# A two-layer hybrid decoder trunk on one core: differential queries and keys also made by units of seven products, heads of attention in two chains, scores begun up to two blocks ahead

## The chip, the core and the metric

The kernel runs on one core of a Trainium2 chip. The metric is the device time of one execution in microseconds (us), median of three runs. The core has a matrix engine (PE; its weight loads are listed apart as PEld), a vector engine (DVE), a scalar engine (ACT), a general engine (POOL, which here mostly issues DMAs) and a sync engine (SP, which issues the weight DMAs). Each works through its own list of instructions in order and waits for the others by semaphores.

## The reference, cut to what matters

512 tokens of width 2048 pass two layers. The change is in the second, where one input projection `z = h @ w_in` is split by columns among two attention groups, and the results, each gated, go through one output projection.

```python
z = h @ w_in                                   # h = rmsnorm(x), (512, 2048)
c_q, c_kv, k_rope, mla_gate, dq, dk, dv, diff_gate = split_cols(z, ODD_SPLITS)
...                                            # 768, 512, 64, 1024, 1024, 1024, 1024, 1024 columns
y_c = causal_mla_attention(q, k_c, v_c) * silu(mla_gate)      # 8 heads
qd = dq.reshape(B, S, 8, 2, 64)
kd = dk.reshape(B, S, 8, 2, 64)
vd = dv.reshape(B, S, 8, 128)
p = softmax(mask(qd @ kd * 64 ** -0.5))        # two maps per head, blocks of 128 queries
a = p[:, 0] - lam * p[:, 1]
od = rmsnorm(a @ vd, subln) * (1 - LAMBDA_INIT)
y_d = od * silu(diff_gate)
return concat([y_c, y_d]) @ w_out
```

## The kernel before

Products are made in a format of 32 bits that keeps fewer bits than float32, so every operand is split into a high and a low part (`high` on ACT, line 256, and `low` on DVE, line 259), and every product is three matmuls (`mm3`, line 273): high by high, high by low, low by high. Weights come in pieces of 128 x 1024 by SP's queue (`Piece`, line 283; tile `wr`), and ACT and DVE split each into `wh` and `wl`, two pieces ahead of their use.

**Jobs.** `Job` (line 373) makes 128 output features for all 512 tokens: the weights are the stationary operand, the split input `X1` (tiles `sh`, `sl`) moves, 16 slices of the contraction with three matmuls each, 48 matmuls of 512 columns into one bank `mm`. The result lies features first. The order of the jobs in layer 1 is that in which lines 1314 to 1370 and 1501 to 1506 make them: five gates of the latent attention (MLA), two units, sixteen jobs of the differential heads, six and four latent jobs, the rotary key, three more gates, and then the jobs of the MLA heads.

**Units.** `Unit` (line 1149) makes 1024 output columns at once, tokens first: the input is stationary (128 tokens), the weights move (512 columns), and six of the eight pairs of contraction slices on either side use seven products in place of eight (Strassen's and Winograd's scheme: sums of weights by DVE in `Sum`, line 330; differences of inputs `TS`, tiles `th`, `tl`, made once in `differences`, line 1111). A unit has 348 matmuls of 512 columns; eight jobs have 384. It holds two banks each of `mm`, `o` and `sc`, and in `first` and `second` (lines 1272, 1283) partial sums are read out before a bank is written again. Before the change units make the values (`vd`) and the gate (`gd`) of the differential heads, which `away` (line 1304) scales and stores to DRAM by POOL's queue.

**Attention.** Each head is a task (`diff`, line 984; `mla`, line 1424), whose few matmuls are put between the matmuls of the jobs. For a block of queries, `scores` makes the scores (tile `sc`), DVE takes the maximum (`softmax_max`, an instruction with `p<-sc,cc`), ACT the exponentials and their sum, DVE scales; then PE transposes the result (`pt<-cc,p`, one of 128 x 128 per block of keys), ACT copies it out (`aT`), and PE multiplies it with the values (`o`). At the end of a differential head, POOL takes a power for the norm (`ssq`), DVE makes `osb`, PE transposes it (`pt<-cc,osb`) and ACT makes `y`. The scores of block n + 1 are made between the exponentials and the scaling of block n (line 1014).

**What sets the order.** A planner (`Plan`, line 74) runs while the program is written: it adds up a cost for each instruction (`pe_cost`, line 115, `act_cost`, `dve_cost`, `dma_cost`), keeps a time at which each tile is ready, and resumes a head's task between two steps of a job (three matmuls) once what it waits for is ready by that reckoning. So PE's, ACT's and DVE's lists are fixed when the program is built; POOL's and SP's are ordered by the framework. Work tiles come from one pool of 76 (`wk`, line 219).

Of the kernel before, what the change touches and what calls it, by code (L numbers as in the profile page):

```python
# [73 lines left out]
class Plan:  # L74
# [40 lines left out]
    def pe_cost(self, op, args, kw):  # L115
        if op == "transpose":
            return 0.108
        rhs = args[2]
        n = _free(rhs)
        if rhs.dtype == F32R:  # L120
            return 0.003 + (n / 2400.0 if n >= 256 else 0.213)
        return 0.006 + max(n, 64) * 4 / 2400.0
# [70 lines left out]
def trunk_kernel(ctx: ExitStack, tc, xT, w0, w0o, wg, w1, w1u, wuq, wuk, wuv, w1o, small, cst, outT):  # L193
# [699 lines left out]
    class Output:  # L893


        def __init__(self, wt, Y, res, sink, count, held=0):
            self.Y, self.YS, self.res, self.xr = Y, [None] * 16, res, {}
            self.next, self.upto, self.gap = 0, 16, 0.0
            self.jobs = [big_job(wt, m, self.YS, self.done(m, sink), self.pre(m), None, (False, m < held))
                         for m in range(count)]  # L900
# [5 lines left out]
        def splitter(self):  # L906
            while self.next < 16:
                k = self.next
                while k >= self.upto or self.Y[k] is None:
                    yield plan.now + 0.4  # L910
                yield after(self.Y[k])
                h, l = wk("yh", F32R), wk("yl", F32R)
                high(h, self.Y[k])
                yield after(h)
                low(l, self.Y[k], h)
                self.YS[k] = h, l
                self.Y[k] = None
                self.next = k + 1
                yield plan.now + self.gap
# [64 lines left out]
    def diff(h, st):  # L984
# [27 lines left out]
        yield from scores(0)  # L1012
        for n in range(NB):
            (pp, sums), nk = res.pop(n), (n + 1) * P
            if n < NB - 1:
                yield from scores(n + 1)
# [31 lines left out]
        Y1[h] = y  # L1048

    def diff_jobs(h):  # L1050
        st = {}

        def fetch():
            for x, src in (("v", vd), ("g", gd)):
                st[x] = wk(x)
                pool.dma_start(st[x], src[h])

        def q_done(acc):
            z = evac(acc, n1, "dq")
            st["q"] = []  # L1060
            plan.spawn(stacks(z, st["q"]))

        def k_done(acc):
            z = evac(acc, n1, "dk")
            lo = [wk("kl", F32R), wk("kl", F32R)]
            a = [wk("kh", F32R), wk("kh", F32R)]
            st["kh"], st["kl"] = a, lo

            def f():
                yield after(z)  # L1070
                for c in range(2):
                    r, s = slice(64 * c, 64 * c + 64), slice(64 - 64 * c, 128 - 64 * c)
                    high(a[c][r], z[r])
                    high(a[c][s], z[r])
                    yield after(a[c])
                    low(lo[c][r], z[r], a[c][r])
                    low(lo[c][s], z[r], a[c][r])
                yield from diff(h, st)
            plan.spawn(f())

        big_job(w1, 2 * h, X1, q_done, fetch, n1)
        big_job(w1, 2 * h + 1, X1, k_done, None, n1)

    MG = [None] * 8

    mgd = dp.tile([8, P, S], F32, name="mgd")[:, :, :]
    vd = dp.tile([8, P, S], F32, name="vd")[:, :, :]
    gd = dp.tile([8, P, S], F32, name="gd")[:, :, :]

    def mla_gate_job(h, away):  # L1090
        def done(acc):
            z = evac(acc, n1, "mg")

            def f():
                yield after(z)
                act.activation(z, z, AF.Silu)
                if away:
                    yield after(z)
                    pool.dma_start(mgd[h], z)
                else:  # L1100
                    MG[h] = z
            plan.spawn(f())
        j = big_job(w1, 16 + h, X1, done, None, n1)
        if h == 0:
            j.pre = lambda: plan.spawn(differences())
# [208 lines left out]
    for h in range(5):  # L1314
        mla_gate_job(h, True)
    Unit(w1u[0], away(vd, AF.Identity))
    Unit(w1u[1], away(gd, AF.Silu))
    for h in range(8):
        diff_jobs(h)
# [47 lines left out]
    LQ = Latent(29, 6, C_QN)  # L1367
    LKV = Latent(25, 4, C_KVN)
    big_job(w1, 24, X1, rope_key_done, None, n1)
    for h in range(5, 8):  # L1370
        mla_gate_job(h, False)
# [52 lines left out]
    def mla(h, st):  # L1424
# [4 lines left out]
        if MG[h] is None:  # L1429
            MG[h] = wk("mg")  # L1430
            pool.dma_start(MG[h], mgd[h])
# [27 lines left out]
        yield from scores(0)  # L1459
        for n in range(NB):  # L1460
            (p, sums), nk = res.pop(n), (n + 1) * P
            if n < NB - 1:
                yield from scores(n + 1)
# [37 lines left out]
    for h in range(8):  # L1501
        if h % 4 == 0:
            rope_jobs(h // 4)
            value_jobs(h // 4)
# [17 lines left out]
    O1 = Output(w1o, Y1, x1d, sink1, 16 - TAIL, 2)  # L1522
# [102 lines left out]
def _tiles1():  # L1625

    cq, ckv, kr, mg, dq, dk, dv, dg = 0, 768, 1280, 1344, 2368, 3392, 4416, 5440
    out = []
    for h in range(8):
        for b in (dq, dk):  # L1630
            out.append(_ranges((b + 128 * h, b + 128 * h + 128)))
# [109 lines left out]
```

## Time and profile before

| what | value |
|---|---|
| median of 3 runs | 1547.8 us (1547.55 to 1548.03) |
| the profiled execution | 1547.16 us |
| its span, first to last instruction | 1545.4 us |
| DVE busy | 935.6 us (61%) |
| ACT busy | 728.6 us (47%) |
| POOL busy | 71.3 us (5%) |
| moved by DMA | 179.75 MB, mean 116 GB/s |
| granted PE clock, mean | 0.997 |

The profile is of one execution; the time outside its span is 1.8 us. Its page gives the busy time of each engine and the chain of work that ended last, and its trace can be asked for groups of instructions, for stretches of time, and for the instructions one by one. A matmul's duration there contains the time from its start until its result is out, so that durations of neighbours overlap; what a matmul costs in a row of them is the distance from start to start.

### The profile page before, as it was taken

What the parts mean: (1) busy time and instruction counts of PE and PEld (TensorE: products, weight loads), DVE (VectorE), ACT (ScalarE), POOL (GpSimd) and SP (SyncE); (2) the same over time, 40 slices, a digit from 0 to 9 for tenths busy, and PEclk for the clock granted to TensorE, in tenths of its full rate; (3) what the DMA queues carried; (4) which work ended last, traced back from release to release, by engine and by line L of the source; (5) the groups of instructions that cost most, each with busy time, mean ns of one, the idle gap of its engine ahead of it and who ended that gap; (6) DMA issues with size and microseconds to landing.
All of it is one profiled execution on the core that took longest, in us unless ns stands there. A gap on an engine that the chain in (4) does not pass through costs nothing.

```text
span 1545.4 us, 19462 instructions
## 1 busy us (share of the span) xinstructions
PE 1529.6 (99%) x7346; PEld 1280.0 (83%) x7346; DVE 935.6 (61%) x1741; ACT 728.6 (47%) x1285; POOL 71.3 (5%) x118
## 2 busy tenths in 40 slices
PE   9999999999999999999999999999999999999996
PEld 7888888888888888878888888888888888888886
DVE  7877676677863445675763677666443466743344
ACT  7465455555652333534433556555333456632222
POOL 0000000000000110000002000000000000010000
PEclk9999999999999999999999999999999999999998
DMA  7223222222334444645636322222232322343323
GB/s 285 85 85 97 85 85 86 89 80 83 95 129 136 152 140 163 222 155 177 210 124 206 101 82 82 96 82 83 83 95 89 98 77 66 111 145 101 99 83 110
DMA packets 59487, 179.75 MB, mean 116 GB/s; under 512 B 7024, under 2 KB 11264, under 8 KB 59264
## 3 DMA queue, kind: packets, MB, share of 16 engines
q1 hardware_dynamic: 51776, 153.84, 31.3%
q0 software_dynamic: 7616, 24.66, 4.7%
q8 instruction: 58, 0.95, 0.3%
q14 instruction: 37, 0.30, 0.1%
HBM read 164.58 MB, written 13.89 MB: 115 GB/s over the span
## 4 chain that ended last, share of the span: by engine, by line
PE 96%; issue 2%; DVE 1%; DMA 0%; ACT 0%; SPq 0%; POOLq 0%; POOL 0%; DVEq 0%; ACTq 0%
PE mm L62 78%; PE sc L62 8%; PE o L62 7%; PE pt L62 3%; DMA xin<-in_xT 0%; DVE st L62 0%; ACT wh L62 0%; DVE s L62 0%; SPq L62 0%; DVE wl L62 0%; DVE sl L62 0%; DVE mg L62 0%; DVE wx L62 0%; POOLq L1736 0%; ACT sh L62 0%
## 5 line engine op out<-in xcount | busy, mean ns | idle before, releaser
L62 DVE TENSOR_TENSOR wl<-wr,wh 128x1024 fp32r<-128x1024 f32 (+1 forms) x236 | 280.9, 1190 | 379.1 <-ACT wh L62 374.7
L62 PE MATMUL mm<-sh,wh 128*128 128x512 f32 x1056 | 419.4, 397 | 0.0
L62 ACT ACTIVATE wh<-wr 128x1024 fp32r<-128x1024 f32 (+1 forms) x236 | 243.8, 1033 | 360.7 <-PE mm L62 252.7
L62 PE MATMUL mm<-sl,wh 128*128 128x512 f32 x1056 | 412.1, 390 | 0.0
L62 PE MATMUL mm<-sh,wl 128*128 128x512 f32 x1056 | 412.1, 390 | 0.0
L62 PEld LDWEIGHTS mm<-sh,wl 128*128 128x128 f32 x1056 | 198.2, 188 | 42.8
L62 PEld LDWEIGHTS mm<-sh,wh 128*128 128x128 f32 x1056 | 198.6, 188 | 36.1
L62 PEld LDWEIGHTS mm<-sl,wh 128*128 128x128 f32 x1056 | 198.8, 188 | 35.5
L62 PE MATMUL mm<-yh,wh 128*128 128x512 f32 x448 | 174.9, 390 | 0.0
L62 PE MATMUL mm<-yl,wh 128*128 128x512 f32 x448 | 174.5, 389 | 0.0
L62 PE MATMUL mm<-yh,wl 128*128 128x512 f32 x448 | 174.4, 389 | 0.0
L62 PEld LDWEIGHTS mm<-yl,wh 128*128 128x128 f32 x448 | 84.1, 188 | 17.4 <-DVE yl L62 0.3
L62 PEld LDWEIGHTS mm<-yh,wh 128*128 128x128 f32 x448 | 84.1, 188 | 17.4
L62 PEld LDWEIGHTS mm<-yh,wl 128*128 128x128 f32 x448 | 84.1, 188 | 17.3
L62 ACT ACTIVATE p<-p,negm 128x128 f32<-128x128 f32 (+3 forms) x96 | 53.8, 560 | 60.0 <-DVE negm L62 58.3
L62 DVE CUSTOM_DVE_ANT_0 p<-sc,cc 128x128 f32<-128x128 f32 (+3 forms) x96 | 46.7, 488 | 41.2 <-PE sc L62 40.8
L62 ACT ACT_TABLE_LOAD x36 | 46.2, 1283 | 1.4 <-PEq L1732 0.7
L62 ACT ACTIVATE sq<-xr 128x512 f32<-128x512 f32 (+1 forms) x33 | 19.3, 586 | 55.0 <-DVE xr L62 55.0
L62 ACT ACTIVATE aT<-pt 128x128 f32<-128x128 f32 (+3 forms) x64 | 27.5, 434 | 36.9 <-PE pt L62 36.4
L62 DVE TENSOR_TENSOR ss<-ss,sq 128x512 f32<-128x512 f32 (+1 forms) x54 | 36.0, 667 | 10.2 <-ACT sq L62 9.4
L62 PE MATMUL mm<-ch,wh 128*128 128x512 f32 x104 | 41.7, 401 | 0.0
L62 PE MATMUL mm<-cl,wh 128*128 128x512 f32 x104 | 40.7, 391 | 0.0
(318 smaller groups left out, 2380.2 us busy)
## 6 DMA issues: line engine op xcount, KB each, us to landing
wr<-in_w SPq DMA_DIRECT2D x134, 512.0 KB, 3.5
wr<-in_w0o SPq DMA_DIRECT2D x32, 512.0 KB, 3.5
wr<-in_w1o SPq DMA_DIRECT2D x32, 512.0 KB, 3.5
wr<-in_w1u SPq DMA_DIRECT2D x30, 512.0 KB, 3.9
wx<-in_w1u SPq DMA_DIRECT2D x40, 256.0 KB, 4.8
wr<-in_wuq SPq DMA_DIRECT2D x12, 384.0 KB, 3.1
xin<-in_xT SPq DMA_DIRECT2D x16, 256.0 KB, 5.2
xr<-in_xT POOLq DMA_DIRECT2D x16, 256.0 KB, 4.0
```

Source lines behind the costliest of these rows:

```text
L62: return f(*args, **kw)
```

## The change

- The queries and keys of the differential heads are made by two more units (`qd`, `kd`), ahead of those for `vd` and `gd`, tokens first, and go to DRAM. The sixteen jobs `diff_jobs` are gone.
- `diff_heads` is a chain of four heads, and two chains run, one begun 8 us after the other by the planner's clock. Each head fetches its `q` and `k` by POOL's queue, and PE transposes them to features first (`pt<-cc,q`, `pt<-cc,k`, four of 128 x 128 each) before they are split as before. The heads now run beside the remaining gates, the rotary key and the latent jobs, whose order is changed, and beside the first value jobs of MLA.
- In both attentions the scores are a task of their own (`ahead`), up to one block ahead in a differential head and up to two in an MLA head.
- A finished differential head `y` goes to DRAM (`y1d`) and is fetched again (`yr`) when the output projection splits it; all eight MLA gates go to DRAM and come back.
- The planner's cost of a matmul is changed: 0.2267 us for 512 columns of the split format (before 0.2163), 0.108 at the least.

On PE, the place where the second unit has ended. The names are bank, moving operand, stationary operand; `sh` and `sl` are the input's two parts, `wh` and `wl` the weight's. Before, the first job of the differential queries:

```order
L62 MATMUL mm_6769<-sh_4000,wh_6702 128x512
L62 MATMUL mm_6769<-sl_4001,wh_6702 128x512
L62 MATMUL mm_6769<-sh_4000,wl_6704 128x512
L62 MATMUL mm_6769<-sh_4071,wh_6702 128x512
L62 MATMUL mm_6769<-sl_4072,wh_6702 128x512
L62 MATMUL mm_6769<-sh_4071,wl_6704 128x512
```

Now, a third unit:

```order
L62 MATMUL mm_6776<-wh_6709,sh_4003 128x512
L62 MATMUL mm_6776<-wl_6710,sh_4003 128x512
L62 MATMUL mm_6776<-wh_6709,sl_4004 128x512
L62 MATMUL mm_6777<-wh_6709,sh_4003 128x512
L62 MATMUL mm_6777<-wl_6710,sh_4003 128x512
L62 MATMUL mm_6777<-wh_6709,sl_4004 128x512
```

The operands have changed sides: the input is stationary now, and two banks take turns.

On PE, a place in the middle of the differential heads, where a block's scores, its transposes and its product with the values stand among the rows of a job. Before:

```order
L62 MATMUL pt_7781<-cc_78,p_7633 128x128 x3
L62 MATMUL sc_7788<-kh_7687,qa_7563 128x256
L62 MATMUL sc_7788<-kl_7685,qa_7563 128x256
L62 MATMUL mm_7670<-sh_5005,wh_7601 128x512
L62 MATMUL mm_7670<-sl_5006,wh_7601 128x512
L62 MATMUL mm_7670<-sh_5005,wl_7603 128x512
L62 MATMUL mm_7670<-sh_5092,wh_7601 128x512
L62 MATMUL mm_7670<-sl_5093,wh_7601 128x512
L62 MATMUL mm_7670<-sh_5092,wl_7603 128x512
L62 MATMUL o_7490<-v_7094,aT_7795 128x128 x3
L62 MATMUL sc_7805<-kh_7688,qb_7564 128x256
L62 MATMUL sc_7805<-kl_7686,qb_7564 128x256
```

Now, at the end of one head while another begins (directly above the first row stand `sc_9869<-kl_9767,qb_9736`, the last scores of the block that `p_9855` belongs to, and one matmul of the job):

```order
L62 MATMUL mm_9774<-sl_4939,wh_9689 128x512
L62 MATMUL mm_9774<-sh_4938,wl_9691 128x512
L62 MATMUL pt_9882<-cc_78,osb_9876 128x128 x4
L62 MATMUL sc_9890<-kh_9768,qa_9735 128x256
L62 MATMUL sc_9890<-kl_9766,qa_9735 128x256
L62 MATMUL mm_9774<-sh_5008,wh_9689 128x512
L62 MATMUL mm_9774<-sl_5009,wh_9689 128x512
L62 MATMUL mm_9774<-sh_5008,wl_9691 128x512
L62 MATMUL mm_9774<-sh_5095,wh_9689 128x512
L62 MATMUL mm_9774<-sl_5096,wh_9689 128x512
L62 MATMUL mm_9774<-sh_5095,wl_9691 128x512
L62 MATMUL pt_9913<-cc_78,p_9855 128x128
```

The rows of two heads now alternate within a few matmuls of the job, and the transposes of a block stand closer behind its scores. From the maxima of its second map to the last scaling, that block's rows stand next to each other in DVE's list, with none of another head or of the weights between.

On POOL, the end of a differential head. `ssq` is the power, `v`, `g`, `q` and `k` are fetches from DRAM. Before:

```order
L62 TENSOR_TENSOR ssq_7746<-ssq_7746,nhalf_79 128x4
L62 DMA v_8218<-vd 128x512
L62 DMA g_8220<-gd 128x512
L62 TENSOR_TENSOR ssq_8031<-ssq_8031,nhalf_79 128x4
L62 DMA v_8497<-vd 128x512
```

Now:

```order
L62 TENSOR_TENSOR ssq_8129<-ssq_8129,nhalf_79 128x4
L62 DMA y1d<-y_8527 128x512
L62 DMA q_8534<-qd 128x512
L62 DMA k_8536<-kd 128x512
L62 DMA v_8599<-vd 128x512
L62 DMA g_8601<-gd 128x512
```

The head's result is stored (`y1d`), and the next head's queries and keys are fetched behind it; of the six fetches of queries that follow a head's end, two stand behind a store of `y` in this way and four ahead of it.

The diff, cut to its core:

```diff
...
         rhs = args[2]
         n = _free(rhs)
         if rhs.dtype == F32R:
-            return 0.003 + (n / 2400.0 if n >= 256 else 0.213)
-        return 0.006 + max(n, 64) * 4 / 2400.0
+            return max(0.108, n * 17 / 38400.0)
+        return 0.002 + max(n, 64) * 4 / 2400.0
     TABLES = {AF.Exp: "e", AF.Sigmoid: "s", AF.Sqrt: "q", AF.Silu: "u"}
...
     class Output:
-        def __init__(self, wt, Y, res, sink, count, held=0):
+        def __init__(self, wt, Y, res, sink, count, held=0, away=0):
             self.Y, self.YS, self.res, self.xr = Y, [None] * 16, res, {}
-            self.next, self.upto, self.gap = 0, 16, 0.0
+            self.next, self.upto, self.gap, self.away = 0, 16, 0.0, away
             self.jobs = [big_job(wt, m, self.YS, self.done(m, sink), self.pre(m), None, (False, m < held))
                          for m in range(count)]
...
                 k = self.next
                 while k >= self.upto or self.Y[k] is None:
                     yield plan.now + 0.4
+                if k < self.away:
+                    y, self.Y[k] = self.Y[k], wk("yr")
+                    pool.dma_start(self.Y[k], y)
                 yield after(self.Y[k])
                 h, l = wk("yh", F32R), wk("yl", F32R)
                 high(h, self.Y[k])
...
                 pp.append(p)
             res[n] = pp, sums
-        yield from scores(0)
+        begun = [0]
+
+        def ahead():
+            for n in range(NB):
+                while n > begun[0] + 1:
+                    yield plan.now + 0.3
+                yield from scores(n)
+
+        plan.spawn(ahead())
         for n in range(NB):
+            while n not in res:
+                yield plan.now + 0.3
             (pp, sums), nk = res.pop(n), (n + 1) * P
-            if n < NB - 1:
-                yield from scores(n + 1)
+            begun[0] = n
             yield after(*pp)
             rr = tiny(2, "rr")
             dve.reciprocal(rr, sums)
...
         y = wk("y")
         act.activation(y, t[0], AF.Identity, scale=subs)
         give("pt", t[0])
-        Y1[h] = y
-
-    def diff_jobs(h):
-        st = {}
-
-        def fetch():
-            for x, src in (("v", vd), ("g", gd)):
+        yield after(y)
+        pool.dma_start(y1d[h], y)
+        Y1[h] = y1d[h]
+
+    qd, kd, vd, gd = (dp.tile([8, P, S], F32, name=x)[:, :, :] for x in ("qd", "kd", "vd", "gd"))
+
+    def diff_heads(hs):
+
+        def fetch(st, h, names):
+            for x in names:
                 st[x] = wk(x)
-                pool.dma_start(st[x], src[h])
-
-        def q_done(acc):
-            z = evac(acc, n1, "dq")
+                pool.dma_start(st[x], {"q": qd, "k": kd, "v": vd, "g": gd}[x][h])
+
+        def features_first(z, out):
+            yield after(z)
+            t = []
+            yield from take("pt", t)
+            transposes(t[0], z, range(NB))
+            yield after(t[0])
+            out.append(t[0])
+
+        for h in hs:
+            st, t = {}, []
+            fetch(st, h, ("q", "k"))
+            yield from features_first(st["q"], t)
             st["q"] = []
-            plan.spawn(stacks(z, st["q"]))
-
-        def k_done(acc):
-            z = evac(acc, n1, "dk")
+            yield from stacks(t[0], st["q"])
+            give("pt", t.pop())
+            fetch(st, h, ("v", "g"))
+            yield from features_first(st["k"], t)
+            z = t.pop()
             lo = [wk("kl", F32R), wk("kl", F32R)]
             a = [wk("kh", F32R), wk("kh", F32R)]
+            for c in range(2):
+                r, s = slice(64 * c, 64 * c + 64), slice(64 - 64 * c, 128 - 64 * c)
+                high(a[c][r], z[r])
+                high(a[c][s], z[r])
+                yield after(a[c])
+                low(lo[c][r], z[r], a[c][r])
+                low(lo[c][s], z[r], a[c][r])
+                yield plan.now
+            give("pt", z)
             st["kh"], st["kl"] = a, lo
-
-            def f():
-                yield after(z)
-                for c in range(2):
-                    r, s = slice(64 * c, 64 * c + 64), slice(64 - 64 * c, 128 - 64 * c)
-                    high(a[c][r], z[r])
-                    high(a[c][s], z[r])
-                    yield after(a[c])
-                    low(lo[c][r], z[r], a[c][r])
-                    low(lo[c][s], z[r], a[c][r])
-                yield from diff(h, st)
-            plan.spawn(f())
-
-        big_job(w1, 2 * h, X1, q_done, fetch, n1)
-        big_job(w1, 2 * h + 1, X1, k_done, None, n1)
+            yield from diff(h, st)
     MG = [None] * 8
+    y1d = dp.tile([8, P, S], F32, name="y1d")[:, :, :]
     mgd = dp.tile([8, P, S], F32, name="mgd")[:, :, :]
-    vd = dp.tile([8, P, S], F32, name="vd")[:, :, :]
-    gd = dp.tile([8, P, S], F32, name="gd")[:, :, :]
-
-    def mla_gate_job(h, away):
+
+    def mla_gate_job(h):
         def done(acc):
             z = evac(acc, n1, "mg")
             def f():
                 yield after(z)
                 act.activation(z, z, AF.Silu)
-                if away:
-                    yield after(z)
-                    pool.dma_start(mgd[h], z)
-                else:
-                    MG[h] = z
+                yield after(z)
+                pool.dma_start(mgd[h], z)
             plan.spawn(f())
-        j = big_job(w1, 16 + h, X1, done, None, n1)
+        j = big_job(w1, h, X1, done, None, n1)
         if h == 0:
             j.pre = lambda: plan.spawn(differences())
...
         return sink
     for h in range(5):
-        mla_gate_job(h, True)
-    Unit(w1u[0], away(vd, AF.Identity))
-    Unit(w1u[1], away(gd, AF.Silu))
-    for h in range(8):
-        diff_jobs(h)
+        mla_gate_job(h)
+    for i, (dst, func) in enumerate(((qd, AF.Identity), (kd, AF.Identity), (vd, AF.Identity), (gd, AF.Silu))):
+        Unit(w1u[i], away(dst, func))
+    first_filler = len(jobs)
     class Latent:
         def __init__(self, base, n, gcol):
...
             KR.extend((h, l))
         plan.spawn(f())
-    LQ = Latent(29, 6, C_QN)
-    LKV = Latent(25, 4, C_KVN)
-    big_job(w1, 24, X1, rope_key_done, None, n1)
     for h in range(5, 8):
-        mla_gate_job(h, False)
+        mla_gate_job(h)
+    big_job(w1, 8, X1, rope_key_done, None, n1)
+    LKV = Latent(9, 4, C_KVN)
+    LQ = Latent(13, 6, C_QN)
+
+    def heads_start():
+        for i in range(2):
+            plan.spawn(diff_heads(range(i, 8, 2)), plan.now + 8 * i)
+    jobs[first_filler].pre = heads_start
     qrs = {}
     VC = {}
...
             yield plan.now + 0.4
         q, k, qr = st["q"], st["k"], qrs.pop(h)
         st.clear()
-        if MG[h] is None:
-            MG[h] = wk("mg")
-            pool.dma_start(MG[h], mgd[h])
+        MG[h] = wk("mg")
+        pool.dma_start(MG[h], mgd[h])
         vc = slice((h % 4) * P, (h % 4 + 1) * P)
         v = [VC[h // 4, n] for n in range(NB)]
         o = []
...
             softmax_exp(p, n, negm, sums)
             res[n] = p, sums
-        yield from scores(0)
+        begun = [0]
+
+        def ahead():
+            for n in range(NB):
+                while n > begun[0] + 2:
+                    yield plan.now + 0.3
+                yield from scores(n)
+
+        plan.spawn(ahead())
         for n in range(NB):
+            while n not in res:
+                yield plan.now + 0.3
             (p, sums), nk = res.pop(n), (n + 1) * P
-            if n < NB - 1:
-                yield from scores(n + 1)
+            begun[0] = n
             yield after(p)
             dve.reciprocal(sums, sums)
             dve.tensor_scalar(p[:, :nk], p[:, :nk], sums, None, ALU.mult)
...
     heads = []
     for h in range(8):
         if h % 4 == 0:
+            value_jobs(h // 4)
             rope_jobs(h // 4)
-            value_jobs(h // 4)
         heads.append(len(jobs))
         mla_jobs(h)
...
             yield from n2.add(xr)
         plan.spawn(post())
-    O1 = Output(w1o, Y1, x1d, sink1, 16 - TAIL, 2)
+    O1 = Output(w1o, Y1, x1d, sink1, 16 - TAIL, 2, 8)
     jobs[heads[5]].pre = lambda: O1.start(16, 1.5)
     def finish(half, parts):
...
 def _tiles1():
-    cq, ckv, kr, mg, dq, dk, dv, dg = 0, 768, 1280, 1344, 2368, 3392, 4416, 5440
+    cq, ckv, kr, mg = 0, 768, 1280, 1344
     out = []
-    for h in range(8):
-        for b in (dq, dk):
-            out.append(_ranges((b + 128 * h, b + 128 * h + 128)))
     for h in range(8):
         out.append(_ranges((mg + 128 * h, mg + 128 * h + 128)))
     out.append(_ranges((kr, kr + 64), (kr, kr + 64)))
...
     w0o = _pack(A(l0_w_out), plain, rows0)
     wg = np.ascontiguousarray(np.concatenate([A(l0_gate_x_w), A(l0_gate_a_w)], axis=2))
     w1 = _pack(A(l1_w_in), _tiles1())
-    w1u = np.stack([_pack_quarters(A(l1_w_in), np.arange(c, c + 1024)) for c in (4416, 5440)])
+    w1u = np.stack([_pack_quarters(A(l1_w_in), np.arange(c, c + 1024)) for c in (2368, 3392, 4416, 5440)])
     rows1 = np.concatenate([np.arange(1024, 2048), np.arange(1024)])
     w1o = _pack(A(l1_w_out), plain, rows1)
     uq = A(l1_w_uq)
```

## The prediction

> **What bounds the kernel now.** I read the page first: engines, slices, chain.
>
> ```profile
> span 1545.4 us, 19462 instructions
> PE 1529.6 (99%) x7346; PEld 1280.0 (83%) x7346; DVE 935.6 (61%) x1741; ACT 728.6 (47%) x1285; POOL 71.3 (5%) x118
> ...
> PEclk9999999999999999999999999999999999999998
> ...
> PE 96%; issue 2%; DVE 1%; DMA 0%; ACT 0%; SPq 0%; POOLq 0%; POOL 0%; DVEq 0%; ACTq 0%
> ```
>
> PE is busy for 99% of the span at a full granted clock, and 96% of the chain that ended last is PE. Busy time alone would prove little, since durations of neighbours overlap; so next I read what PE waited for, over the whole run (columns: total us, times, longest).
>
> ```profile
> PE pt L62 <- DVE dg L62: 1.8, 1, 1.8
> PE sc L62 <- DVE s L62: 1.3, 4, 0.4
> PE sc L62 <- DVE junk L62: 1.1, 1, 1.1
> PE pt L62 <- ACT sq L62: 0.8, 1, 0.8
> PE o L62 <- DVE sl L62: 0.5, 2, 0.3
> PE mm L62 <- DVE yl L62: 0.3, 1, 0.3
> ```
>
> That is all: 5.8 us. None of it belongs to the sixteen jobs of queries and keys or to a softmax. So the kernel ends when PE has worked through its list, and a change is worth what it takes out of that list, less the waits that it brings in. Work that leaves or joins another engine counts only by such waits.
>
> **The price of a row.** From the chain, in order of time (start, us, what):
>
> ```profile
> 672.37 2.72 PE mm L62 x12
> ...
> 903.42 6.14 PE mm L62 x27
> ...
> 910.83 0.44 PE pt L62 x4
> ```
>
> Twelve matmuls of 512 columns in a unit take 2.72 us, 0.2267 each; 27 in a job take 6.14, 0.2274 each. Four transposes among the heads displace 0.44 us, 0.11 each.
>
> **Queries and keys out of jobs, into units.** Sixteen jobs of 48 matmuls go: 768 x 0.2267 = 174.1 us (174.6 at the job's price). Two units of 348 come. What a unit takes with its waits shows in the two that are there: the first matmul of each, and the first of the job behind them.
>
> ```profile
> 664.56 0.50 PE L62 MATMUL mm<-wh,sh 128*128 128x512 f32 x1
> ...
> 745.04 0.50 PE L62 MATMUL mm<-wh,sh 128*128 128x512 f32 x1
> ...
> 824.61 0.39 PE L62 MATMUL mm<-sh,wh 128*128 128x512 f32 x1
> ```
>
> 80.5 and 79.6 us, 160.1 together, where 696 x 0.2267 would be 157.8: a unit loses about 1.1 us, in the waits `sc <- DVE s` above (two a unit) and where it takes over its banks. New units keep the same rows around these points, so I let them cost the same: 174.1 - 160.1 = **14.0 us saved** (14.6 with the job's price; 16.3 if the new units lost nothing). What feeds a unit is DVE's and ACT's splitting and SP's weights:
>
> ```profile
> 656.00:735.00 79.00, 78.24 (x343) 63.80 (x342) 51.42 (x73) 31.91 (x46) 4.09 (x6) 1.00 0.53 171
> 735.00:815.00 80.00, 79.33 (x348) 64.74 (x347) 54.16 (x76) 33.47 (x48) 6.54 (x9) 1.00 0.52 168
> ```
>
> The columns are PE, PEld, DVE, ACT and POOL busy with counts, PE's clock, DMA share and GB/s. In the second unit, which also carries the first one's results away, DVE is busy for 54 of 80 us and the DMA engines for 52%. It is no slower than the first, so two more in a row should not fall behind either.
>
> **Transposes.** Eight heads have four for q and four for k: 64 x 0.11 = **7.0 us added**. They stand on PE's list and nothing hides them. A group stands whole among matmuls of a job, as `osb` did.
>
> One rule speaks against this. The Trainium skill, "TensorE: Matmul & The Clock Gate", section "Part 4: PE-mode transpose", gives some 275 ns for a transpose of 128 x 128 in a kernel and says that the array does not count as busy during it. By that, 64 would be an estimated 17.6 us. The chain above disagrees with it as a price in a row, at 0.11 us each, though the duration of one agrees:
>
> ```profile
> L62 PE MATMUL pt<-cc,osb 128*128 128x128 f32 x32 | 4.9, 275 | 0.0
> ```
>
> 275 ns from start to result; in a row the next one starts long before that.
>
> **The fetch of q.** Two of the six later fetches stand on POOL behind the store of the last head's `y`, which waits for ACT. On PE there stand, from the end of that head's `osb` transposes to the new `pt<-cc,q`, 19 matmuls of 512 columns, 3 transposes and 3 fp32 products (two passes of 0.11): 4.31 + 0.33 + 0.66 = 5.3 us. Needed are ACT's `y`, POOL's issue of the store, and a fetch like that of `v`:
>
> ```profile
> L62 ACT ACTIVATE y<-pt,subs x8: 669/688/691, 911.3 to 1089.3; 128x512 f32<-128x512 f32 x8
> ...
> L62 POOL DMA_DIRECT2D x1d<-xr x16 | 8.7, 547 | 168.3 <-DVE xr L62 168.3
> ...
> DMA to landing us min/median/max: 2.9/4.2/5.6
> ```
>
> 0.69 + 0.55 + 4.2 = 5.4 us, between 4.1 and 6.8; so PE waits 0.1 us in the middle, at most 1.5, twice: **0.3 us** (0 to 3). The four other fetches need not wait for `y`, the keys stand 2 us and more further down, and the first two heads' queries were asked for while a unit still ran.
>
> On this fetch the Trainium skill, "DMA: Bandwidth & Descriptors", section "Anatomy of one DMA — SWDGE (gpsimd) path", fits about 2.0 us plus bytes over 436 GB/s, which for 256 KB is an estimated 2.6 us. The wait would then be nothing. No fetch of `v` here was that fast, so the row is used.
>
> **Two chains, scores ahead, another planner cost.** These move rows on PE and neither add nor take any. Their cost is waits that are not there now. The planner had taken a matmul for 0.2163 us where it takes 0.2267, so all that it scheduled came 5% later on PE than it reckoned; that cushion is gone. Counting PE's rows at the prices above between a block's last scores and its transposes, the middle one of 64 blocks has 10.1 us before and 5.4 now, the shortest 3.8 and 2.7. The shortest is shown with the change. Its needs, for 128 keys:
>
> ```profile
> L62 DVE CUSTOM_DVE_ANT_0 p<-sc,cc 128x128 f32<-128x128 f32 x24 | 6.9, 286 | 5.9 <-PE sc L62 5.8
> L62 DVE DVE_READ_ACCUMULATOR2_ANT negm<- 128x1 f32 x160 | 13.3, 83 | 0.0
> L62 ACT ACTIVATE p<-p,negm 128x128 f32<-128x128 f32 x24 | 9.6, 399 | 14.1 <-DVE negm L62 14.0
> L62 ACT ACTIVATION_READ_ACCUMULATOR p<-p,negm 128x1 f32 x96 | 17.9, 187 | 0.0
> L62 DVE RECIPROCAL rr<-sums 128x2 f32<-128x2 f32 x32 | 5.1, 160 | 0.1
> L62 DVE TENSOR_TENSOR rr<-rr,lam 128x1 f32<-128x1 f32 x32 | 5.1, 160 | 1.1
> L62 DVE TENSOR_SCALAR p<-p,rr 128x128 f32<-128x128 f32 x8 | 2.3, 286 | 0.3
> L62 DVE SCALAR_TENSOR_TENSOR p<-p,rr,p 128x128 f32<-128x128 f32 x8 | 2.8, 351 | 0.3
> ...
> L62 DVE TENSOR_TENSOR wl<-wr,wh 128x1024 fp32r<-128x1024 f32 x216 | 263.9, 1222 | 353.3 <-ACT wh L62 348.9 <-PE o L62 4.3
> ```
>
> 1.9 us of work in 2.7 us of PE: enough for four hops between engines, not for a split of weights (1.22 us) ahead of it on DVE. Such a place would wait about 0.5 us, and behind a waiting PE stands everything. I take **0.8 us** in all, a few such places among 64; the bounds are 0 and about 6 us (0.1 us at every block). The end of a head, from its last product through `ssq` and `osb` to the transposes, has 3.2 us at the least now and 3.4 before, where it just sufficed: **0.4 us** (0 to 1).
>
> **A wait that goes.** Before the output projection's last rows PE waited for the last MLA head:
>
> ```profile
> 1371.56 0.49 PE L62 MATMUL mm<-yh,sh 128*128 128x512 f32 x1
> 1372.33 0.50 PE L62 MATMUL mm<-yl,sh 128*128 128x512 f32 x1 [0.27 <-DVE yl L62]
> ```
>
> 0.77 us from start to start where the pitch is 0.23: about 0.5 us lost. The heads now end further ahead of the rows that use them (3.2 us of PE at least, 1.4 before), so **0.5 us** goes. PE's own list is what is late next there. The store and fetch of `y` lie tens of microseconds ahead of `yh`; three more table loads on ACT lie beside PE.
>
> **The sum**, against the profiled execution's 1547.16 us: -14.0 + 7.0 + 0.3 + 0.8 + 0.4 - 0.5 = -6.0, so 1541.2. The median of the runs shown is 0.6 above that execution; I say **1541.5 us**. With every bound at its good end it is -16.3 + 7.0 - 0.5 = -9.8 (1537.4), at its bad end -14.0 + 7.0 + 3 + 6 + 1 = +3 (1550).
>
> **The rivals.** *Softmax waits* (13 in 100): PE meets its transposes too early in both attentions. For it speaks the halved distance; against it that not one such wait is listed now, and that DVE is busy for 61%. At 0.1 us a block, 64 blocks give 6.4 us: 1547, no change. Slower would take over 0.15 us a block.
>
> *Transposes cost their duration* (4): 64 x 0.275 = 17.6 in place of 7.0, so 1541.2 + 10.6 = 1552, slower. It decides from 0.2 us a transpose on. The chain's 0.44 us for four speaks against it. The skill's page named above would have it so.
>
> *Units fall behind* (7): four in a row hold three pairs of banks and take work tiles for sums, results and stores at once. If each new unit lost 3 us more, the end would be 1547.5. Against it speaks the second unit's 79.6 us.
>
> *The saving is not there* (3): if the moving and the stationary operand's change of side mattered, a unit's price would show it, and it does not: 0.2267 against 0.2274.
>
> **How the numbers follow.** The forecast's own case has 73 in 100, between 1538.5 and 1544.5. The range of 8 in 10 takes in most of the first rival and of the third: 1538.5 to 1547.5. About 0.2% (3.1 us) is what a measurement can tell from no change. Faster by more: the forecast and a part of the softmax waits, 0.78. Same: most of the rest of the two rivals, 0.14. Slower: 0.08.
>
> **What would show it.** Right: two more pairs of waits `sc <- DVE s`; units of 80 us each; four transposes of q in 0.44 us in the chain; no wait of `pt` for `p` over a few tenths. Wrong: PE's list of waits with `pt <- DVE p` or `pt <- DMA q` of several us in all, or the third and fourth unit longer than the second.

## The result and the profile after

| | before | after |
|---|---|---|
| median | 1547.67 us (1547.11 to 1548.03) | 1558.2 us (1557.65 to 1558.65, 4 runs) |
| ratio | 1 | 1.007, 95% interval 1.0057 to 1.0083 |
| the profiled execution | 1547.16 us, span 1545.4 | 1557.92 us, span 1556.2 |

The changed kernel is slower by 10.5 us; the forecast was 6 us faster. Its page, the same lines as shown of before:

```profile
span 1556.2 us, 19845 instructions
PE 1527.0 (98%) x7338; PEld 1273.2 (82%) x7338; DVE 995.3 (64%) x1845; ACT 758.5 (49%) x1352; POOL 104.1 (7%) x172
...
PE 85%; DVE 6%; issue 4%; ACT 3%; DMA 1%; SPq 0%; POOL 0%; POOLq 0%; DVEq 0%; ACTq 0%
```

PE is busy for 2.6 us less than before in a span that is 10.8 us longer, and the chain that ended last has lost 11 points of PE to DVE, ACT and issue. So the list of PE did get shorter; PE stands still in it more often. Where, shows the stretch from the first head's start to the middle of the latent heads. The columns are PE, PEld, DVE, ACT and POOL busy with counts, PE's clock, DMA share and GB/s. Before:

```profile
986.00:1260.00 274.00, 274.00 (x1317) 229.47 (x1317) 147.74 (x295) 126.86 (x238) 9.42 (x12) 1.00 0.29 89
```

After:

```profile
986.00:1260.00 274.00, 263.15 (x1358) 219.31 (x1357) 194.16 (x466) 170.32 (x385) 37.37 (x58) 0.99 0.36 113
```

PE was never idle there and is now idle for 10.9 of 274 us. What it waited for, over the whole run (total us, times, longest):

```profile
PE o L62 <- ACT aT L62: 6.0, 4, 2.0
PE pt L62 <- DVE p L62: 2.7, 4, 1.5
PE sc L62 <- DVE s L62: 2.6, 8, 0.4
PE pt L62 <- DMA q<-qd: 2.0, 1, 2.0
...
PE mm L62 <- DVE qn L62: 0.6, 2, 0.5
```

The third row is the forecast one: two more units, four more such pairs. The first, second and fourth are new, 10.7 us. Nine waits cause them, not many small ones. The costliest are for `aT`, ACT's copy of a block's transposes, which no step of the prediction names. ACT itself was held up (its own list of waits, and then ACT, DVE and PE in order of time at the largest of the four; in square brackets the idle time and what ended it):

```profile
ACT kh L62 <- DVE kl L62: 17.5, 7, 3.3
```

```profile
1052.22 1.20 ACT L62 ACTIVATE kh<-pt 64x512 fp32r<-64x512 f32 x2 [0.22 <-PE pt L62]
...
1053.29 0.68 DVE L62 TENSOR_TENSOR qa<-pt,qa 64x512 fp32r<-64x512 f32 x1
...
1054.71 0.69 DVE L62 TENSOR_TENSOR kr<-mm,rstd 128x512 f32<-128x512 f32 x1
...
1055.32 1.37 DVE L62 TENSOR_TENSOR kl<-pt,kh 64x512 fp32r<-64x512 f32 x2
...
1056.72 1.20 ACT L62 ACTIVATE kh<-pt 64x512 fp32r<-64x512 f32 x2 [3.31 <-DVE kl L62]
1057.95 2.54 ACT L62 ACTIVATE krs<-kr 32x512 f32<-32x512 f32 x4
1060.52 0.60 ACT L62 ACTIVATE aT<-pt 128x512 f32<-128x512 f32 x1
1061.17 0.60 PE L62 MATMUL o<-v,aT 128*128 128x128 f32 x3 [2.04 <-ACT aT L62]
```

This is to be read from the bottom. PE waits 2.04 us for `aT`. ACT comes to `aT` late, because it stood for 3.31 us ahead of the second pair of high parts of the keys, `kh<-pt`. That pair reads nothing that DVE writes. It waits for DVE's first pair of low parts, `kl<-pt,kh`, which only **reads the same tile** `pt`. Two more of the four waits for `aT`, at 1171 and 1194 us, stand behind such a wait of ACT, of 3.29 and 2.69 us. Before, the keys were split from a work tile (`dk`) and no such wait was there; a head of the kernel before, whose low parts begin while the high parts still run:

```profile
930.31 2.59 ACT L62 ACTIVATE kh<-dk 64x512 fp32r<-64x512 f32 x4
...
931.75 2.80 DVE L62 TENSOR_TENSOR kl<-dk,kh 64x512 fp32r<-64x512 f32 x4
```

The Trainium skill, "PSUM — Partial Sum Buffer", section "PSUM bank collisions raise a hardware error", has it that two engines may not be on one bank and 32-partition quadrant at once, reads against reads included, so software must keep them apart. By the code the two pairs read different partitions of `pt` (0 to 63 the low parts, 64 to 127 the high ones), so that rule alone does not ask for this wait: the program as built keeps the readers of the whole tile apart. No run here tries a narrower order. The trace shows them kept apart seven times, with ACT idle for 17.5 us in all.

The longest wait for `p` comes the same way, by turns: ACT waits for DVE, and then DVE for ACT, with the scaling of `p` queued behind on DVE.

```profile
1011.81 1.20 ACT L62 ACTIVATE kh<-pt 64x512 fp32r<-64x512 f32 x2 [1.97 <-DVE kl L62]
...
1013.04 1.40 DVE L62 TENSOR_TENSOR kl<-pt,kh 64x512 fp32r<-64x512 f32 x2 [1.27 <-ACT kh L62]
...
1015.25 0.48 DVE L62 SCALAR_TENSOR_TENSOR p<-p,rr,p 128x256 f32<-128x256 f32 x1
...
1015.79 0.44 PE L62 MATMUL pt<-cc,p 128*128 128x128 f32 x2 [1.54 <-DVE p L62]
```

This one cost PE more than its 1.54 us. The windows around it:

```profile
1013.00:1016.42 3.42, 1.72 (x10) 0.96 (x8) 3.20 (x9) 1.86 (x7) 0.00 (x0) 1.00 0.01 5
1016.42:1019.83 3.41, 3.41 (x11) 3.02 (x12) 2.34 (x6) 1.13 (x5) 0.00 (x0) 0.50 0.35 95
1019.83:1023.24 3.41, 3.41 (x17) 2.84 (x16) 1.00 (x4) 3.36 (x5) 0.55 (x1) 1.00 0.15 59
```

In the first stretch PE is busy for 1.72 of 3.42 us. Right behind it the granted clock is 0.50 for 3.41 us, and two matmuls that follow each other start 0.43 us apart (1017.20 and 1017.63) in place of 0.23; then it is 1.00 again. By these numbers the stretch at half clock loses an estimated 1.7 us, half of 3.41. That PE is listed as busy there hides the loss.

The fetch of `q` that PE waited for, in the chain (start, us, what):

```profile
1042.73 0.50 POOL y1d L62
...
1043.31 5.61 DMA q<-qd
...
1049.05 0.64 PE pt L62 x4
```

### The profile page after: what moved, and what is told of

It reads as the page before. It is cut to its first block, busy times and chain, and to the rows that moved or that the text cites. A ratio compares the mean times of both kernels' runs of the same rounds, so it can differ in the third digit from the quotient of the medians.

```text
span 1556.2 us, 19845 instructions
## 1 busy us (share of the span) xinstructions
PE 1527.0 (98%) x7338; PEld 1273.2 (82%) x7338; DVE 995.3 (64%) x1845; ACT 758.5 (49%) x1352; POOL 104.1 (7%) x172
## 4 chain that ended last, share of the span: by engine, by line
PE 85%; DVE 6%; issue 4%; ACT 3%; DMA 1%; SPq 0%; POOL 0%; POOLq 0%; DVEq 0%; ACTq 0%
PE mm L62 62%; PE sc L62 10%; PE o L62 10%; PE pt L62 3%; DVE wl L62 1%; ACT wh L62 1%; DVE p L62 1%; DVE kl L62 1%; DMA xin<-in_xT 0%; DVE s L62 0%; ACT qr L62 0%; DMA q<-qd 0%; ACT L62 0%; ACT kh L62 0%; DVE st L62 0%
## 5 line engine op out<-in xcount | busy, mean ns | idle before, releaser
L62 PE MATMUL mm<-sh,wh 128*128 128x512 f32 x800 | 320.8, 401 | 0.0
L62 PE MATMUL mm<-sl,wh 128*128 128x512 f32 x800 | 312.8, 391 | 0.0
L62 PE MATMUL mm<-sh,wl 128*128 128x512 f32 x800 | 312.7, 391 | 0.0
L62 PEld LDWEIGHTS mm<-sh,wl 128*128 128x128 f32 x800 | 150.3, 188 | 32.9
L62 PEld LDWEIGHTS mm<-sh,wh 128*128 128x128 f32 x800 | 151.0, 189 | 25.8
L62 PEld LDWEIGHTS mm<-sl,wh 128*128 128x128 f32 x800 | 151.1, 189 | 25.2
L62 PEld LDWEIGHTS mm<-yh,wl 128*128 128x128 f32 x448 | 84.1, 188 | 17.6
L62 ACT ACTIVATE p<-p,negm 128x384 f32<-128x384 f32 (+3 forms) x96 | 53.4, 556 | 34.1 <-DVE negm L62 31.6
L62 DVE CUSTOM_DVE_ANT_0 p<-sc,cc 128x384 f32<-128x384 f32 (+3 forms) x96 | 46.1, 486 | 15.9 <-PE sc L62 15.2
L62 DVE TENSOR_TENSOR wl<-wx,wh 128x512 fp32r<-128x512 f32 x56 | 36.2, 688 | 28.1 <-ACT wh L62 28.1
L62 PE MATMUL sc<-wh,sh 128*128 128x512 f32 x112 | 44.5, 397 | 2.6 <-DVE s L62 2.6
```

The costliest lines, as they stand in the source:

```text
L62: return f(*args, **kw)
```

## The experiments

Three theories came first. **A, the shared bank**: ACT and DVE are put in order on the tile `pt`, and this holds ACT's list up, and so `aT` and `p`. **B, the cushion**: the planner's new cost of a matmul sets dependent rows nearer to each other on PE, without the margin that the old cost left. **C, density**: two chains bring too many rows of heads together. Each of the first four experiments changes one thing in the changed kernel. Each batch of runs measured the kernel before anew; ratios are to that.

**The high parts first.** All four high parts of a head's keys on ACT, then all four low parts on DVE, from the same tile:

```diff
-            for c in range(2):
-                r, s = slice(64 * c, 64 * c + 64), slice(64 - 64 * c, 128 - 64 * c)
+            rs = [(slice(64 * c, 64 * c + 64), slice(64 - 64 * c, 128 - 64 * c)) for c in range(2)]
+            for c, (r, s) in enumerate(rs):
                 high(a[c][r], z[r])
                 high(a[c][s], z[r])
-                yield after(a[c])
+            yield after(*a)
+            for c, (r, s) in enumerate(rs):
                 low(lo[c][r], z[r], a[c][r])
                 low(lo[c][s], z[r], a[c][r])
```

> The keys' split writes all four high parts on ACT before the four low parts on DVE; nothing else differs from the changed kernel (1558.2 us). Theory A (shared bank: ACT's second pair of high parts waits in line for DVE's first pair of low parts, since both read one PSUM bank, and all that stands behind on ACT comes late): ACT waits for `kl` go from 17.5 us to none, PE's waits `o <- ACT aT` from 6.0 to under 1.5, 1547 to 1550 us; the wait for the fetch of q (2 us) stays. Theory B (the planner's new matmul cost took its cushion away): over 1556. Theory C (two chains are too dense for DVE and ACT): over 1556.

Measured: 1548.88 us (1547.58 to 1550.49), ratio 1.0006 (0.9997 to 1.0016): 9.3 us less than the change, with the same instructions. ACT's wait for `kl` is gone, and PE's list has changed so:

```profile
PE pt L62 <- DMA q<-qd: 2.4, 1, 2.4
...
PE pt L62 <- DVE p L62: 0.9, 2, 0.4
...
PE o L62 <- ACT aT L62: 0.4, 1, 0.4
```

The waits for `aT` went from 6.0 to 0.4 and those for `p` from 2.7 to 0.9, 7.4 us together. So they came from the order on the bank, as A has it; the softmax itself is not too slow. The wait for `q`, 2.4 us here, has a stretch of 3.41 us at half clock at its end, from 1046.4 us on.

**Copy first.** ACT copies the transposed queries and keys into a work tile, gives the bank back, and both are split from the copy: 16 more ACT instructions.

```diff
             yield after(t[0])
-            out.append(t[0])
+            zc = wk("zc")
+            act.activation(zc, t[0], AF.Copy)
+            give("pt", t[0])
+            yield after(zc)
+            out.append(zc)
```

> ACT copies the transposed queries and keys out of PSUM into work tiles and both are split from there, in the old order; 16 copies of about 0.6 us join ACT. Theory A: the wait of ACT for `kl` is gone although the order of the split is that of the changed kernel, 1547 to 1552 us. Theories B and C: over 1557, since ACT has more work than before.

Measured: 1546.85 us (1546.29 to 1547.17), ratio 0.9992 (0.9983 to 1.0001): 11.35 us less than the change, though ACT does more. In the stretch that lost 10.9 us:

```profile
986.00:1260.00 274.00, 271.41 (x1433) 228.81 (x1432) 202.14 (x491) 187.32 (x422) 39.19 (x59) 1.00 0.36 116
```

PE stands still for 2.6 us there, of which 1.5 are the fetch of `q`. ACT is busy there for 17 us longer than in the change (the copies, and work that now comes earlier), and that costs nothing: what its list had lost was time in waiting. Two lines by engine show the old order of the split on a work tile, ACT and DVE side by side as in the kernel before:

```profile
1055.73 2.60 ACT L62 ACTIVATE kh<-zc 64x512 fp32r<-64x512 f32 x4
...
1056.40 1.38 DVE L62 TENSOR_TENSOR kl<-zc,kh 64x512 fp32r<-64x512 f32 x2
```

This kernel is 2 us faster than the one before. Of the 3.7 us between the two profiled spans, 2.6 are a wait for `q` shorter by 0.9 us and the stretch at half clock, which is not there (1.7 us); that the queries too are split from a copy may add to it, and that is not shown.

**The old planner cost** in the changed kernel (`pe_cost` as before, the rest as after).

> The changed kernel with the planner's old cost of a matmul (0.2163 us for 512 columns), so all that it schedules stands 5% later on PE. Theory A: ACT's waits for `kl` stay and PE's waits shrink only by what the cushion covers: 1553 to 1558 us. Theory B: 1545 to 1548, with no wait of PE for `aT` or `p` left. Theory C: over 1556.

Measured: 1556.4 us (1554.77 to 1559.21), ratio 1.0057 (1.0042 to 1.0072). The interval meets the change's own, so B is not the main cause. ACT's wait and the fetch are still there. PE's waits for `aT` fall to 2.5 us and those for `p` to 0.3, so the margin hides much of what ACT's wait does; but the waits for `q` and `qn` grow by 3.4 us together, and a stretch of 3.41 us at half clock follows one of 2.41 us for `q`:

```profile
ACT kh L62 <- DVE kl L62: 19.8, 8, 4.2
```

```profile
PE pt L62 <- DMA q<-qd: 3.7, 2, 2.4
...
PE o L62 <- ACT aT L62: 2.5, 1, 2.5
PE mm L62 <- DVE qn L62: 2.3, 1, 2.3
```

**One chain** of eight heads in place of two of four.

```diff
-        for i in range(2):
-            plan.spawn(diff_heads(range(i, 8, 2)), plan.now + 8 * i)
+        plan.spawn(diff_heads(range(8)), plan.now)
```

> The changed kernel with the eight differential heads in one chain. Theory A: ACT waits for `kl` stay at about 2 us a head, fewer rows of another head stand behind them: 1552 to 1559 us. Theory B: over 1556. Theory C: 1545 to 1549, PE's waits for `aT` and `p` gone, unless the chain ends too late for the output projection, which would show as a wait of PE for `yh`.

Measured: 1588.52 us, ratio 1.0263 (1.0246 to 1.028), far above what A and C expected; B's "over 1556" takes it in, and B falls by the runs above. The last differential head ends at 1389 us, where in the change it ends at 1226; one chain is too slow to be done while there are jobs to stand beside:

```profile
1260.00:1400.00 140.00, 114.64 (x661) 96.53 (x660) 96.62 (x268) 83.55 (x215) 21.50 (x38) 0.92 0.28 89
```

PE is idle for 25 of 140 us there (7.5 of them in one wait for `yh`), and the clock falls to 0.92. That is the case that the expectation had set aside for C, and the rest of C's sign did not come: PE still waits 6.7 us for `aT` and 8.9 for `p`. Two chains are needed to end in time, and this run says nothing on how close they may stand. Against C speak the two runs without turns on the bank: two chains as in the change, and these waits all but gone.

What was left after A: e2's kernel takes 1546.85 where the forecast would have 1541. Two theories. **D**: a few tight places, the fetch of `q` and those that the planner's cushion had covered. **E**: the units or the transposes cost more than their terms. Two runs on the changed kernel and two parts of the change alone in the kernel before followed.

**Copy first, and the fetch earlier**: the next head's `q` and `k` are asked for when the last block of a head is taken up, ahead of the store of `y`.

```diff
             begun[0] = n
+            if n == NB - 1 and ending:
+                ending()
...
-            fetch(st, h, ("q", "k"))
...
-            yield from diff(h, st)
+            nxt.clear()
+            ending = None if i + 1 == len(hs) else lambda g=hs[i + 1]: fetch(nxt, g, ("q", "k"))
+            yield from diff(h, st, ending)
```

> e2_copy_first, and each head's queries and keys are asked for when the last block of the head before it in its chain comes to its scaling, some 5 us earlier than now. Theory D (what is left of the lost time in e2_copy_first is single waits at places set too tight, the fetch of q of 1.5 us among them): 1544.5 to 1546, no wait of PE for `q`. Theory E (units and transposes cost more in rows than I priced them): no more than 0.3 us below e2_copy_first, that is 1546.5.

Measured: 1545.93 us (1545.45 to 1548.08) beside 1547.25 of before in that batch, ratio 0.9992 (0.9984 to 1.0001). The wait of 1.5 us for `q` is gone from the list, and the time moves by less than a microsecond; against the kernel before of each batch it is 0.4 us.

**The same with the old planner cost.**

> As f1_copy_qearly, with the planner's old cost of a matmul, so that every dependent row stands about 5% further behind on PE. Theory D: the remaining tight places (first layer 0.8 us, `qn` 0.6 us, `p` 0.7 us) go too: 1541.5 to 1543.5. Theory E: no better than f1_copy_qearly, 1545 or more.

Measured: 1544.85 us (1543.48 to 1546.18), ratio 0.9983 (0.9975 to 0.9992). It is **faster than both kernels**: 13.35 us under the change, 2.4 under before. The stretch is full again,

```profile
986.00:1260.00 274.00, 273.99 (x1449) 231.77 (x1448) 203.64 (x494) 186.94 (x422) 38.31 (x59) 1.00 0.35 117
```

and no wait for `aT`, `p` or `q` is listed. It missed D's expectation by 1.35 us and lies 0.15 under E's; this list shows a part of what remains:

```profile
PE sc L62 <- DVE s L62: 2.6, 8, 0.4
PE mm L62 <- DVE qn L62: 2.3, 1, 2.3
```

The second wait stands at 1319 us: `qn` is what reads a bank out that PE's next job wants, and on DVE it stands behind `qa` and `qb`, 0.7 us each. With the new cost the list has 0.6 for it.

**The new planner cost alone**, in the kernel before.

> The kernel before with only the planner's new cost of a matmul. PE's rows are the same in number. Theory D: tight places appear, 0.5 to 3 us slower than before, 1548.2 to 1550.5. Theory E: the same as before, 1547.4 to 1548.

Measured: 1552.41 us (1551.36 to 1553.12), ratio 1.0031 (1.0019 to 1.0044): 5.2 us slower with the same instructions, more than D had. The largest place, in PE's list and in two windows:

```profile
PE mm L62 <- ACT yh L62: 1.5, 1, 1.5
```

```profile
1374.78:1378.19 3.41, 1.68 (x9) 1.11 (x8) 1.38 (x2) 0.63 (x1) 0.54 (x1) 1.00 0.29 77
1378.19:1381.60 3.41, 3.41 (x9) 2.65 (x8) 1.50 (x2) 1.58 (x2) 0.00 (x0) 0.50 0.00 0
```

One wait of 1.5 us, and behind it again 3.41 us at half clock, an estimated 1.7 us lost: 3.2 us of the 5.2 together. The other 2 were not traced. So the old cost, though false by 5%, was a cushion worth microseconds in the old kernel, and about 1 in the new (1545.93 against 1544.85).

**The scores ahead alone**, in the kernel before.

> The kernel before with only the scores as a task of their own, up to one block ahead in a differential head and two in an MLA head. Both theories: within 0.7 us of before, 1547 to 1548.4; D allows a few tenths either way by the places that move.

Measured: 1546.42 us (1545.92 to 1546.93), ratio 0.9994 (0.9985 to 1.0003): 0.8 us less than before in that batch, at the edge of what can be told.

**The transposes twice**, in the kernel of 1544.85: each group of four transposes of queries or keys is written a second time into the same bank, 64 transposes more.

```diff
             transposes(t[0], z, range(NB))
+            transposes(t[0], z, range(NB))
```

> Copy first, keys and queries fetched early, old planner cost (that kernel took 1544.85), and here each of the 16 groups of four transposes of q and k is made twice into the same bank: 64 transposes more. Transposes at their price in a row (0.11 us each): +7.0, so 1550 to 1553.5, groups of eight in 0.87 us, and the +7.0 of the prediction stands. Transposes at their duration (0.275 us each): +17.6, so 1561 or more, groups of eight in 2.2 us. Theory that what is missing of the forecast saving lies in the transposes: something between, 1555 to 1559.

Measured: 1551.1 us (1550.22 to 1552.49), ratio 1.0025 (1.0015 to 1.0036). That is 6.3 us for 64, 0.10 us each. In the chain a group of eight displaces twice what four do:

```profile
990.09 0.87 PE pt L62 x8
```

**The scores as before**, in the kernel of 1544.85.

> The same kernel of 1544.85, with the scores of both attentions made as before (block n + 1 between the exponentials and the scaling of block n) and no task ahead. Theory that scores ahead save waits in this kernel as they did alone in the kernel before (1.3 us there): 1545.5 to 1547.5. Theory that they put the transposes of a block too close behind its scores and cost the last few us of the forecast: 1540.5 to 1543.

Measured: 1549.15 us (1548.58 to 1550.3), ratio 1.0013 (1.0004 to 1.0022): 4.3 us slower. (The 1.3 us in the expectation set the run of the kernel before against another batch; in its own batch it is 0.8.) What comes in:

```profile
PE mm L62 <- ACT yh L62: 1.9, 2, 1.5
...
PE mm L62 <- DVE sums L62: 1.6, 1, 1.6
...
PE mm L62 <- DVE yl L62: 0.8, 3, 0.3
```

Heads that make their scores late end late, and the output projection waits for them. So scores ahead earn their place in the new kernel, by more than the first theory had; the theory that they put the transposes too close falls.

## Why the prediction was wrong, step by step

**The units: right, but for 0.8 us.** The first matmul of the first unit, the matmuls with which the four units take up their second bank, and the first of the job behind the last:

```profile
665.08 0.39 PE L62 MATMUL mm<-wh,sh 128*128 128x512 f32 x1
...
666.02 0.50 PE L62 MATMUL mm<-wh,sh 128*128 128x512 f32 x1
...
746.49 0.50 PE L62 MATMUL mm<-wh,sh 128*128 128x512 f32 x1
...
826.93 0.50 PE L62 MATMUL mm<-wh,sh 128*128 128x512 f32 x1
...
907.38 0.50 PE L62 MATMUL mm<-wh,sh 128*128 128x512 f32 x1
...
986.94 0.39 PE L62 MATMUL mm<-sh,wh 128*128 128x512 f32 x1
```

From second bank to second bank it is 80.5, 80.4 and 80.5 us. The prediction took such a matmul for the unit's first, but three matmuls of the first bank stand ahead of it (in the kernel before, the first ones start at 663.61 and 744.18), so its 79.6 us leaves 0.9 us of the last unit out. From first to last, four units take 321.9 us, two 160.9 and not 160.1, and the saving is 13.2 and not 14.0. The rival of units that fall behind is out, and so is that of a saving that isn't there.

**The transposes: right.** Forecast 7.0 us at 0.11 each; 64 more of them cost 6.3. The rival by duration (0.275 each, 17.6 in all) is out. Theory E falls with these two: the terms -14.0 and +7.0, which make the change worth doing, held within 1 us, and their small errors cancel.

**The fetch of `q`: too small.** Forecast 0.3 us, "at most 1.5, twice"; PE waited once, 2.0 us. The fetch took 5.6 us, the far end of the row used, not 4.2. Asking earlier moved the time by under 1 us, so this term was a small part of the miss. The fit of the Trainium skill, "DMA: Bandwidth & Descriptors", section "Anatomy of one DMA — SWDGE (gpsimd) path", by which the prediction estimated 2.6 us, is further off still.

**Softmax waits: right in size, once the bank is out of the way.** The forecast had 0.8 us in all. The change shows 2.7 in waits for `p`, but 0.9 or less once the bank holds no engine up, and none is listed in the fastest kernel. What stood ahead of these last 0.9 us on DVE was not traced. The rival had them at every block, for nearness; the nine waits of the change are few and long and come from elsewhere.

**The output projection's wait: right.** Neither `yh` nor `yl` is in the list of the change. The scores ahead do that: taken out, 2.7 us of such waits come back.

**The planner's cost: under-priced.** The prediction saw that the cushion goes, priced it together with the rest, and at 0.8 us. Alone it costs the kernel before 5.2 us; taken back it gives 1.8 in the change, within the intervals, and 1.1 in the kernel with copies.

**The failed step** is the one on transposes: "They stand on PE's list and nothing hides them" priced them on PE alone. What they leave behind was taken from the description of the change, by which queries and keys "are split as before". The order of the split is as before, its source is not. Before, the source of the split was a work tile; in the change it is a bank of PSUM that ACT and DVE read in turns, and the diff says so in `out.append(t[0])`. The prediction's own rule, that work on another engine counts "only by such waits", was right, but no wait was looked for here, and what is queued on ACT behind `kh`, the copies `aT` that PE waits for, was not named. It measured 9.3 us by reordering and 11.35 by copying, of the 16.7 us between forecast and result. Both runs also move rows elsewhere in the lists, which alone can be worth microseconds (5.2 in the run of the new cost); tied to the bank are ACT's 17.5 us of waits, all gone, and 7.4 us of PE's. Of the signs of being wrong that the prediction names, PE's list of waits came, with `p` at 2.7 and `q` at 2.0 us; the largest wait, for `aT`, is not among them. For this split the prediction counted what the change puts on PE and asked of ACT and DVE at most how busy they are. With DVE at 64% and ACT at 49% the answer sounds safe; ACT's stall is idle time, and busy time doesn't show it.

The rest, in the kernel with copies, early fetch and old cost: 2.4 us under before, where the prediction had 6. Of these 3.6 us the wait for `qn` is 2.3, and the units' term was 0.8 too large. What is left was not traced to single places and stays open, as does how near to each other the two chains could stand.

## What to carry to other kernels

When a tile moves from SBUF to PSUM, look at every engine that reads it, not only at who writes it: readers that ran side by side may now run in turns. Where two engines must read one bank, let one finish all its reads before the other begins, or copy the tile out at once; 16 copies of 0.6 us on ACT cost nothing here and gave back 11 us. And correct a planner's false cost only together with a new margin, since other parts may live on the error.

## What the runs showed of the hardware

At or just behind the end of some waits of PE the granted clock was 0.50 for 3.41 us, with matmuls 0.43 us apart in place of 0.23, an estimated 1.7 us lost each time. The waits were 1.54 us in the change, 1.5 in the run of the new cost alone, and 2.4 with the high parts first and with the old cost. The Trainium skill, "TensorE: Matmul & The Clock Gate", section "HAM oscillation — how this bites in real kernels", puts the abstract rule at idle gaps of over about 3.4 us. Shorter waits were enough here, though PE was idle more than once around the first two (a further 0.16 and 0.22 us). Other waits, of 2.04 us for `aT` at 1061 among them, left the clock at 1.00:

```profile
1060.00:1064.00 4.00, 2.83 (x16) 2.50 (x17) 1.77 (x2) 2.51 (x5) 0.00 (x0) 1.00 0.02 4
```

So a wait of this length costs its own time or about 1.7 us more, and which of the two it is can't be read from its length. What decides it, these runs do not show.
